# Rotary products on POOL, taken one in each step of the attention and put behind DVE's normalisation

## The chip, the cores and the metric

The kernel runs on one NeuronCore of a Trainium2 chip. It is one launch, and the metric is the device time of that launch in microseconds (us). Five engines work beside each other and wait for each other through semaphores: TensorE (PE in the profile), VectorE (DVE), ScalarE (ACT), GpSimd (POOL) and SyncE (SP), which issues the DMAs. Each engine takes its instructions in the order in which the program gives them to it.

## What is computed

The reference is an encoder block on 1024 tokens of width 1024 with two attention branches of eight heads each, a gate for each, and a squared-ReLU MLP. The change touches the windowed attention, in whose queries and keys the first 16 of each head's 64 values are rotated:

```python
qb = partial_rotary(qb.reshape(B, S, SWA_Q_HEADS, HEAD_DIM), pos)
kb = partial_rotary(kb.reshape(B, S, SWA_KV_HEADS, HEAD_DIM), pos)
y_na = neighbourhood_attention(qa, ka, va, na_rpb[l]) @ w_branch_na[l]
y_swa = windowed_gqa_with_sink(qb, kb, vb, swa_sink[l]) @ w_branch_swa[l]
mixed = jax.nn.sigmoid(ga) * y_na + jax.nn.sigmoid(gb) * y_swa
attn_out = mixed @ w_out[l] + b_out[l]
h = layer_norm(DEEPNORM_ALPHA * h + attn_out, ln1_g[l], ln1_b[l])
u = jnp.square(jax.nn.relu(h @ w_ff1[l] + b_ff1[l]))
h = layer_norm(DEEPNORM_ALPHA * h + u @ w_ff2[l] + b_ff2[l], ln2_g[l], ln2_b[l])
```

The rotation of a vector x is x * cos + swap(x) * sin, where swap exchanges the two halves of the 16 values.

## The kernel before

The work is held with channels on the 128 partitions and tokens along the free dimension. Products that need more than one pass of TensorE's number format are made of three matmuls, of a rounded part and a rest (names with hi or h, and lo or l). All engines run an order that is written by hand: the program text issues each instruction to its engine, and nothing moves it later.

**Steps.** The attention is a row of 64 steps, four for each of the 16 heads; a step is 256 queries, as two blocks of 128 queries against 256 or 384 keys. The first eight heads are the windowed ones. The work of a step is spread over three turns of the loop in `steps`, so that each engine always has something of another step at hand. Turn s issues, in this order:
- `part_a2` for step s + 1: DVE adds the sink to the sum of the exponentials (L563), takes the reciprocal (L564), and normalises the two blocks `ss` in place (L567, twice, 128x256 or 128x384);
- `part_a` for step s + 2: TensorE makes the two blocks of scores in a PSUM bank each (L530, L531; there are two such banks), DVE adds the mask and takes the row's maximum, writing the block `ss` (L533, twice, and a short read of the result each), and a small operation of two columns makes the bias of the exponential from it (L539);
- `part_b` for step s: TensorE transposes the normalised blocks, ACT rounds them to `pth` (L591), and DVE makes the rest `ptl` (L594). Between these two, `part_e` for step s + 2 lets ACT make the exponentials in place (L551, twice) and that of the sink (L554);
- `part_c` for step s - 1: TensorE multiplies with the values. In every second turn ACT (L630) and DVE (L631) bring the sum out of PSUM as `oT`.

**Fill.** Between these parts, `pump` gives TensorE matmuls of the projections (L278) that later heads need: 12 groups of three in each turn for the first eight heads. A list `later` holds what has to follow a projection; `defer` puts an entry on it with a number of groups to wait, and `flush` issues those that are due. The weights' rest (`wlo`, L486, DVE) and rounded part (`whi`, L481, ACT) come that way too.

**Rotary.** `rope` follows a half (512 tokens) of the projection of keys or of a pair of query heads. ACT brings it out of PSUM as `qf` (L393). Then `turn` issues four operations in a row: on DVE the swap, `stream_shuffle` into `qs` (L398), and on POOL the two products and the addition, each of 128x512 (L399, L400, L401). Some groups later `hi` (ACT, L437 for queries) and `lo` (DVE, L442, two instructions) make the rounded part and the rest. There are ten halves: two of the keys and two for each of four pairs of query heads. Five of them are turned ahead of the steps, and five inside them: the second half of the second pair, and both halves of the third and fourth. `qs` has one buffer (it shares the tag `vt`), and `qf` alternates between two.

POOL has nothing else to do in this stretch. Behind the steps here come the eight heads of neighbourhood attention, the gates, the output projection and the MLP.

Of the kernel before, what the change touches and what calls it, by code (L numbers as in the profile page):

```python
# [10 lines left out]
F32 = mybir.dt.float32  # L11
F32R = mybir.dt.float32r
AF = mybir.ActivationFunctionType
ALU = mybir.AluOpType

P = 128
# [62 lines left out]
SWAP = [(i + 8) % 16 if i < 16 else i for i in range(32)]  # L79
# [3 lines left out]
def encoder_block(ctx, tc, x, w_in, w_br, w_out, w_ff1, w_ff2, par, rows, rpbp,  # L83
                  ident_d, masks_d, rope_d, out):
    nc = tc.nc
    PE, ACT, DVE, POOL = nc.tensor, nc.scalar, nc.vector, nc.gpsimd

    def b32(ap):
        return ap.bitcast(F32)


    cp = ctx.enter_context(tc.tile_pool(name="const", bufs=1))
# [65 lines left out]
    ap = actx.enter_context(tc.tile_pool(name="ap", bufs=2, reuse_waits="tile"))  # L158
# [126 lines left out]
    def defer(*fns, pe=False):  # L285

        later.append([fns[0], fns[1:], pe])
# [75 lines left out]
    rt = ap.tile([P, 2, S], F32, tag="vv", name="rt")  # L363
# [17 lines left out]
        return bias_of  # L381

    n_rope = [0]

    def rope(ps, bias, half, then, late=D_ROPE):
        cs = slice(half * 512, (half + 1) * 512)
        b = []

        def evac():
            tag = ("x2", "wlo2")[n_rope[0] % 2]  # L390
            n_rope[0] += 1
            b.append((ap if tag == "x2" else wp).tile([P, 512], F32, tag=tag, name="qf", bufs=1))
            ACT.activation(b[0], ps, AF.Identity, bias=bias, scale=1.0)  # L393

        def turn():
            qf = b[0]
            qs = ap.tile([P, 512], F32, tag="vt", name="qs", bufs=1)
            DVE.stream_shuffle(qs, qf, SWAP)  # L398
            POOL.tensor_tensor(out=qf, in0=qf, in1=rt[:, 0, cs], op=ALU.mult)  # L399
            POOL.tensor_tensor(out=qs, in0=qs, in1=rt[:, 1, cs], op=ALU.mult)  # L400
            POOL.tensor_tensor(out=qf, in0=qf, in1=qs, op=ALU.add)  # L401
        hi, lo = then
        defer(0, evac, late[0], turn, late[1], lambda: hi(b[0]), late[2], lambda: lo(b[0]))

    def proj_swa_k(w, store):
        khs = [ap.tile([P, S], F32R, tag="kh", name="kh") for _ in range(2)]
        kls = [ap.tile([P, S], F32R, tag="kl", name="kl") for _ in range(2)]
        store.append((khs, kls))
        for half in range(2):
            ps = psum("mm")  # L410
            yield from gemm3_steps(ps, w, lambda part, k: h_perm(part, k, half))

            def hi(kf, half=half):
                for i in range(2):
                    a, b = slice(i * 64, i * 64 + 64), slice(64 - i * 64, 128 - i * 64)
                    ACT.copy(nat(khs[i][a], half), grp(kf[a]))
                    ACT.copy(nat(khs[i][b], half), grp(kf[a]))

            def lo(kf, half=half):
                for i in range(2):  # L420
                    a, b = slice(i * 64, i * 64 + 64), slice(64 - i * 64, 128 - i * 64)
                    DVE.tensor_tensor(out=nat(kls[i][a], half), in0=grp(kf[a]), in1=nat(b32(khs[i][a]), half),
                                      op=ALU.subtract)
                    DVE.tensor_copy(nat(kls[i][b], half), nat(b32(kls[i][a]), half))
            rope(ps, prm[:, C_KB:C_KB + 1], half, (hi, lo))

    def proj_swa_q(hp, w, store):
        qs = [ap.tile([P, S], F32R, tag="q", name="q", bufs=3) for _ in range(2)]
        store.extend(qs)
        for half in range(2):  # L430
            ps = psum("mm")
            yield from gemm3_steps(ps, w, lambda part, k: h_perm(part, k, half))

            def hi(qf, half=half):
                for i in range(2):
                    a = slice(i * 64, i * 64 + 64)
                    ACT.copy(nat(qs[i][a], half), grp(qf[a]))  # L437

            def lo(qf, half=half):
                for i in range(2):  # L440
                    a, b = slice(i * 64, i * 64 + 64), slice(64 - i * 64, 128 - i * 64)
                    DVE.tensor_tensor(out=nat(qs[i][b], half), in0=grp(qf[a]), in1=nat(b32(qs[i][a]), half),  # L442
                                      op=ALU.subtract)
            rope(ps, prm[:, C_QB + hp:C_QB + hp + 1], half, (hi, lo), D_ROPE2 if hp else D_ROPE)
# [111 lines left out]
    def part_a2(s):  # L556
        if s >= 64:
            return
        hd, t = heads[s // 4], s % 4
        pns, st = hd.pairs[t]  # L560
        sink_h = hd.get()[4]
        if sink_h is not None:
            DVE.tensor_tensor(out=st[:, 4:6], in0=st[:, 4:6], in1=st[:, 6:8], op=ALU.add)  # L563
        DVE.reciprocal(out=st[:, 6:8], in_=st[:, 4:6])  # L564
        for i in range(2):
            p, n, c0 = pns[i]
            DVE.tensor_scalar(out=p[:, :n], in0=p[:, :n], scalar1=st[:, 6 + i:7 + i], scalar2=None, op0=ALU.mult)  # L567

    def part_b(s, between):

        hd, t = heads[s // 4], s % 4
        pns = hd.pairs[t][0]

        order = []
        for c in range(max(2 * t - 1, 0), min(2 * t + 3, 8)):
            for i in range(2):
                if abs(2 * t + i - c) <= 1:
                    order.append((c, i))
        pth = ap.tile([P, 6, P], F32R, tag="pth", name="pth")
        ptl = ap.tile([P, 6, P], F32R, tag="ptl", name="ptl")  # L580
        cut = 3 if order[0][0] == 2 * t - 1 else 2
        pts = []
        for a, b in ((0, cut), (cut, len(order))):
            pt = psum("t")
            for u in range(a, b):
                c, i = order[u]
                p, n, c0 = pns[i]
                PE.transpose(pt[:, (u - a) * P:(u - a + 1) * P], p[:, (c - c0) * P:(c - c0 + 1) * P], ident)  # L588
            pts.append((a, b, pt[:, :(b - a) * P].rearrange("p (u f) -> p u f", f=P)))
        for a, b, pv in pts:  # L590
            ACT.copy(pth[:, a:b, :], pv)  # L591
        between()
        for a, b, pv in pts:
            DVE.tensor_tensor(out=ptl[:, a:b, :], in0=pv, in1=b32(pth[:, a:b, :]), op=ALU.subtract)  # L594
        hd.pairs[t] = order, pth, ptl
# [71 lines left out]
    with tc.manual_schedule(engines=MANUAL):  # L667
# [38 lines left out]
        for i in range(2 * NK + LAG + HB):  # L706
# [27 lines left out]
            for (h, w), lag in lags:  # L734
                j = i - lag - h * NK
# [15 lines left out]
        def steps(s, n, before_b=None, before_c=None):  # L751

            part = [int(n * SPLIT[0]), int(n * SPLIT[1])]
            part.append(n - sum(part))
            if 0 <= s + 1 < 64:
                part_a2(s + 1)
            if s + 2 < 64:
                part_a(s + 2)
            pump(part[0])
            if before_b:  # L760
                before_b()
            if 0 <= s < 64:
                part_b(s, lambda: part_e(s + 2))
            elif s < 0:
                part_e(s + 2)
            flush(False)
            pump(part[1])
            if before_c:
                before_c()
            if s >= 1:  # L770
                part_c(s - 1)
            flush()
            pump(part[2])
# [10 lines left out]
        def s1_sum(i):  # L784

            DVE.tensor_tensor(out=g1, in0=b32(hT[:, 0, K1, T2]) if i == 0 else g1,
                              in1=b32(hT[:, 0, K2, T2] if i == 0 else hT[:, 1, (K1, K2)[i - 1], T2]), op=ALU.add)
        counts = [CNT[0]] * 8 + [CNT[1]] * 8
        heads_w = []

        def head_w0(p):
# [390 lines left out]
    ops = {}  # L1182
# [840 lines left out]
```

## Time and profile before

| what | us |
|---|---|
| median of three runs (lowest, highest) | 1349.87 (1348.58, 1350.26) |
| the profiled execution, its own time | 1348.45 |
| its span on the core | 1346.7 |
| TensorE busy | 1321.3 |
| DVE busy | 993.5 |
| ACT busy | 707.4 |
| POOL busy | 278.9 |
| first and last shuffle L398 start | 53.6 and 178.9 |

A row of the timeline gives the start in us from the span's start, the time that the instruction took, the engine, the line, the operation, the tile that it writes and those that it reads, shapes and types, and how many were merged; in brackets stands how long the engine was idle before it and what ended that. Where two instructions are merged, the time is that from the start of the first to the end of the second. The ends of neighbours on one engine can overlap by about 0.1 us. A row of a list of waits gives who waited for whom, the us in total, the number of times, and the longest.

### The profile page before, as it was taken

How to read it: one execution, taken by the hardware profiler on the slowest of the kernel's cores; microseconds unless marked ns; L12 is line 12 of the kernel's file. 1: busy time of each engine (PE TensorE's matmuls, PEld its weight loads, DVE VectorE, ACT ScalarE, POOL GpSimd, SP SyncE). 2: the span in 40 equal slices, each digit the busy share in tenths (PEclk: the TensorE clock that was granted, in tenths of full speed). 3: DMA queues.
4: the chain of work that ended last, by engine and by line, in shares of the span. 5: the costliest groups of instructions: out<-in, count | busy, mean ns of one | idle time of the engine just before them, and what ended most of it. 6: DMA issues, size and time to landing. Idle time of an engine off the chain costs nothing.

```text
span 1346.7 us, 17318 instructions
## 1 busy us (share of the span) xinstructions
PE 1321.3 (98%) x6296; PEld 1087.7 (81%) x6296; DVE 993.5 (74%) x1617; ACT 707.4 (53%) x1230; POOL 278.9 (21%) x264
## 2 busy tenths in 40 slices
PE   8999999999999999999999999999999999999997
PEld 6788778888888878888888788888888888888785
DVE  7758988877777896443678977677655767787778
ACT  6446666766665545542446755555555533333346
POOL 4351121121120000334630012222100001011207
PEclk9999999999999999999999999999999999999999
DMA  6511111111101332655233566655628644544323
GB/s 230 196 69 48 48 51 41 38 38 44 38 23 39 126 126 103 214 195 198 79 141 133 179 228 203 211 194 181 207 99 304 219 188 149 211 148 176 121 102 125
DMA packets 66422, 183.94 MB, mean 137 GB/s; under 512 B 10400, under 2 KB 12064, under 8 KB 60576
## 3 DMA queue, kind: packets, MB, share of 16 engines
q1 hardware_dynamic: 65904, 182.38, 39.1%
q8 instruction: 49, 0.80, 0.2%
q10 hardware_dynamic: 432, 0.46, 0.1%
q14 instruction: 37, 0.30, 0.1%
HBM read 126.69 MB, written 56.31 MB: 136 GB/s over the span
## 4 chain that ended last, share of the span: by engine, by line
PE 73%; DVE 15%; ACT 7%; issue 2%; POOL 1%; DMA 1%; SPq 0%; DVEq 0%; ACTq 0%; POOLq 0%
PE ps_mm L278 10%; PE ps_mm L1746 6%; PE ps_o L1313 6%; PE ps_s L1746 6%; PE ps_t L1313 6%; PE ps_mm L1313 6%; PE ps_o L1746 5%; PE ps_t L1746 5%; ACT ss L551 3%; DVE ss L567 3%; PE ps_s L1313 2%; DVE ss L533 2%; PE ps_mm L851 1%; PE ps_o L624 1%; PE ps_t L588 1%
## 5 line engine op out<-in xcount | busy, mean ns | idle before, releaser
L278 PE MATMUL ps_mm<-hT,whi 128*128 128x512 f32 x832 | 270.0, 398 | 5.3 <-DVE kl L355 2.6
L278 PEld LDWEIGHTS ps_mm<-hT,whi 128*128 128x128 f32 x832 | 152.9, 188 | 35.3 <-DVE kl L355 4.6
L278 PE MATMUL ps_mm<-hT,wlo 128*128 128x512 f32 x416 | 166.9, 401 | 1.0 <-DVE wlo L684 1.0
L551 ACT ACTIVATE ss<-ss,st 128x384 f32<-128x384 f32 (+1 forms) x128 | 74.5, 585 | 79.9 <-DVE st L539 48.4
L1612 ACT CAST t<-stg 128x2048 fp32r<-128x2048 f32 x28 | 53.4, 1908 | 84.0 <-PE ps_o L1746 47.0
L1765 POOL TENSOR_TENSOR acc<-acc,rst 128x512 f32<-128x512 f32 x16 | 29.5, 1843 | 297.9 <-DMA rst<-xr_d 285.0
L1746 PE MATMUL ps_mm<-t,t 128*128 128x512 f32 x384 | 91.0, 392 | 0.0
L1746 PE MATMUL ps_s<-t,t 128*128 128x512 f32 x384 | 90.8, 392 | 0.0
L278 PEld LDWEIGHTS ps_mm<-hT,wlo 128*128 128x128 f32 x416 | 78.3, 188 | 12.2 <-DVE wlo L684 1.5
L1746 PEld LDWEIGHTS ps_mm<-t,t 128*128 128x128 f32 x384 | 72.1, 188 | 16.3
L1746 PEld LDWEIGHTS ps_s<-t,t 128*128 128x128 f32 x384 | 72.1, 188 | 16.1
L1313 PE MATMUL ps_t<-hS,tw 128*128 128x512 f32 x348 | 84.3, 391 | 0.0
L591 ACT CAST pth<-ps_t 128x384 fp32r<-128x384 f32 (+1 forms) x128 | 51.8, 455 | 52.5 <-PE ps_t L588 51.6
L1313 PEld LDWEIGHTS ps_t<-hS,tw 128*128 128x128 f32 x348 | 65.3, 188 | 14.3
L1615 DVE TENSOR_TENSOR t<-stg,t 128x2048 fp32r<-128x2048 f32 x28 | 65.5, 2338 | 13.1 <-ACT t L1612 13.1
L1135 POOL TENSOR_TENSOR mx<-sg 128x512 f32<-128x512 f32 x16 | 33.5, 2092 | 189.9 <-DVE sg L1134 189.9
L1746 PE MATMUL ps_t<-t,t 128*128 128x512 f32 x288 | 68.6, 392 | 0.4 <-DVE t L1615 0.3
L1746 PE MATMUL ps_o<-t,t 128*128 128x512 f32 x288 | 67.8, 391 | 0.0
L594 DVE TENSOR_TENSOR ptl<-ps_t,pth 128x384 fp32r<-128x384 f32 (+1 forms) x128 | 61.1, 518 | 7.0 <-ACT pth L591 6.8
L1746 PEld LDWEIGHTS ps_t<-t,t 128*128 128x128 f32 x288 | 53.9, 188 | 13.1 <-DVE t L1615 1.3
L1746 PEld LDWEIGHTS ps_o<-t,t 128*128 128x128 f32 x288 | 54.1, 188 | 11.8
L1589 POOL TENSOR_TENSOR rst<-rst,rr 128x512 f32<-128x512 f32 x16 | 22.6, 1412 | 190.7 <-DMA rst<-xn_d 190.7
(306 smaller groups left out, 3170.5 us busy)
## 6 DMA issues: line engine op xcount, KB each, us to landing
us_d<-usl SPq DMA_DIRECT2D x112, 256.0 KB
stg<-us_d SPq DMA_DIRECT2D x28, 1024.0 KB
raw<-in_w_ff SPq DMA_DIRECT2D x36, 512.0 KB
raw<-in_w_in SPq DMA_DIRECT2D x28, 512.0 KB
sg<-sg_d SPq DMA_DIRECT2D x32, 256.0 KB
w2b<-in_w_ff SPq DMA_DIRECT2D x7, 1024.0 KB
w2a<-in_w_ff SPq DMA_DIRECT2D x5, 1024.0 KB
sg_d<-sa SPq DMA_DIRECT2D x16, 256.0 KB
```

The costliest lines, as they stand in the source:

```text
L278: PE.matmul(ps, a[:, k, :], act(b, k), start=(k == 0 and i == 0), stop=(k == NK - 1 and i == 2))
L533: DVE.tensor_tensor_reduce(out=p[:, :n], in0=ps[:, :n], in1=bias_of(j), scale=1.0, scalar=NEG, op0=ALU.add, op1=ALU.max, accum_out=st[:, i ...
L551: ACT.activation(p[:, :n], p[:, :n], AF.Exp, bias=st[:, 2 + i:3 + i], scale=0.125, accum_out=st[:, 4 + i:5 + i])
L567: DVE.tensor_scalar(out=p[:, :n], in0=p[:, :n], scalar1=st[:, 6 + i:7 + i], scalar2=None, op0=ALU.mult)
L591: ACT.copy(pth[:, a:b, :], pv)
L594: DVE.tensor_tensor(out=ptl[:, a:b, :], in0=pv, in1=b32(pth[:, a:b, :]), op=ALU.subtract)
L1135: POOL.tensor_tensor(out=mx[:, f, half * 512:(half + 1) * 512], in0=both[0], in1=both[1], op=ALU.add)
L1313: PE.matmul(ps, ww, act[:, part, k, :], start=(first and k == 0 and m == 0), stop=(k == 3 and m == 2), skip_group_check=True)
L1612: ACT.copy(slot[:, :, 0, :], src)
L1615: DVE.tensor_tensor(out=slot[:, :, 1, :], in0=src, in1=b32(slot[:, :, 0, :]), op=ALU.subtract)
L1746: PE.matmul(ps, st[:, a, part, j * P:(j + 1) * P], w[:, a, wpart, :], start=(first and a == 0 and m == 0), stop=(a == 3 and m == 2), skip_ ...
L1765: POOL.tensor_tensor(out=z, in0=z, in1=t, op=ALU.add)
```

## The change

Inside the steps, `turn` no longer issues its four operations at once. It puts five entries on a list `rope_ops`: the shuffle, the two products, the addition, and an entry that defers `hi` and `lo`. If the list holds nothing else, the shuffle is issued at once. At the end of each `part_a2` the new function `rope_step` takes one product or addition from the list. Ahead of it stands a copy on POOL of one column of the block that DVE normalised last, into a small tile `junk`, so POOL's queue waits there for the second L567 of that step. After an addition, `hi` is deferred by 4 groups, and if a second half is on the list, its shuffle by 8. Ahead of the steps the order is as it was.

```diff
--- before.py
+++ after.py
@@ -381,6 +381,18 @@
         return bias_of
 
     n_rope = [0]
+    in_steps, rope_ops = [], []
+
+    def rope_step(p):
+
+        if rope_ops:
+            j = cp.tile([P, 1], F32, tag="junk", name="junk", bufs=2)
+            POOL.tensor_copy(j, p[:, 0:1])
+            rope_ops.pop(0)()
+            if len(rope_ops) % 5 == 1:
+                rope_ops.pop(0)()
+                if rope_ops:
+                    defer(8, rope_ops.pop(0))
 
     def rope(ps, bias, half, then, late=D_ROPE):
         cs = slice(half * 512, (half + 1) * 512)
@@ -394,13 +406,25 @@
 
         def turn():
             qf = b[0]
-            qs = ap.tile([P, 512], F32, tag="vt", name="qs", bufs=1)
-            DVE.stream_shuffle(qs, qf, SWAP)
-            POOL.tensor_tensor(out=qf, in0=qf, in1=rt[:, 0, cs], op=ALU.mult)
-            POOL.tensor_tensor(out=qs, in0=qs, in1=rt[:, 1, cs], op=ALU.mult)
-            POOL.tensor_tensor(out=qf, in0=qf, in1=qs, op=ALU.add)
+            qs = []
+
+            def shuffle():
+                qs.append(ap.tile([P, 512], F32, tag="vt", name="qs", bufs=1))
+                DVE.stream_shuffle(qs[0], qf, SWAP)
+            ops = [shuffle,
+                   lambda: POOL.tensor_tensor(out=qf, in0=qf, in1=rt[:, 0, cs], op=ALU.mult),
+                   lambda: POOL.tensor_tensor(out=qs[0], in0=qs[0], in1=rt[:, 1, cs], op=ALU.mult),
+                   lambda: POOL.tensor_tensor(out=qf, in0=qf, in1=qs[0], op=ALU.add),
+                   lambda: defer(4 if in_steps else late[1], lambda: hi(qf), late[2], lambda: lo(qf))]
+            if in_steps:
+                rope_ops.extend(ops)
+                if len(rope_ops) == 5:
+                    rope_ops.pop(0)()
+            else:
+                for op in ops:
+                    op()
         hi, lo = then
-        defer(0, evac, late[0], turn, late[1], lambda: hi(b[0]), late[2], lambda: lo(b[0]))
+        defer(0, evac, late[0], turn)
 
     def proj_swa_k(w, store):
         khs = [ap.tile([P, S], F32R, tag="kh", name="kh") for _ in range(2)]
@@ -565,6 +589,7 @@
         for i in range(2):
             p, n, c0 = pns[i]
             DVE.tensor_scalar(out=p[:, :n], in0=p[:, :n], scalar1=st[:, 6 + i:7 + i], scalar2=None, op0=ALU.mult)
+        rope_step(p)
 
     def part_b(s, between):
 
@@ -786,6 +811,7 @@
             DVE.tensor_tensor(out=g1, in0=b32(hT[:, 0, K1, T2]) if i == 0 else g1,
                               in1=b32(hT[:, 0, K2, T2] if i == 0 else hT[:, 1, (K1, K2)[i - 1], T2]), op=ALU.add)
         counts = [CNT[0]] * 8 + [CNT[1]] * 8
+        in_steps.append(1)
         heads_w = []
 
         def head_w0(p):
```

Lines after the change have other numbers: L398 to L401 become L413 and L415 to L417, L442 becomes L466, L486 L510, L533 L557, L539 L563, L563 and L564 L587 and L588, L567 L591, L594 L619, and L631 L656. So an L563 in the rows of the change is the small operation that makes the bias.

POOL's queue at the sixth and seventh half, the first ones inside the steps, before:

```order
L399 TENSOR_TENSOR qf<-qf,rt 128x512
L400 TENSOR_TENSOR qs<-qs,rt 128x512
L401 TENSOR_TENSOR qf<-qf,qs 128x512
L399 TENSOR_TENSOR qf<-qf,rt 128x512
L400 TENSOR_TENSOR qs<-qs,rt 128x512
L401 TENSOR_TENSOR qf<-qf,qs 128x512
```

and with the change:

```order
L390 COPY junk<-ss 128x1
L415 TENSOR_TENSOR qf<-qf,rt 128x512
L390 COPY junk<-ss 128x1
L416 TENSOR_TENSOR qs<-qs,rt 128x512
L390 COPY junk<-ss 128x1
L417 TENSOR_TENSOR qf<-qf,qs 128x512
L390 COPY junk<-ss 128x1
L415 TENSOR_TENSOR qf<-qf,rt 128x512
```

The order of the products is the same; a copy that reads `ss` stands ahead of each of the fifteen. They go into the steps 1 to 3, 7 to 12 and 15 to 20, counted by the step that is normalised.

DVE's queue where the second half of the third pair of query heads is swapped (`wlo` is a weight's rest, `oT` the output of a head), the end of one step and the end of the next, before:

```order
L539 TENSOR_SCALAR st<-st,snk_101 128x2
L594 TENSOR_TENSOR ptl<-ps_t,pth 128x384
L594 TENSOR_TENSOR ptl<-ps_t,pth 128x256
L398 STREAM_SHUFFLE qs<-qf 128x512
L563 TENSOR_TENSOR st<-st 128x2
L564 RECIPROCAL st<-st 128x2
```

and one step later on DVE:

```order
L539 TENSOR_SCALAR st<-st,snk_101 128x2
L594 TENSOR_TENSOR ptl<-ps_t,pth 128x256
L594 TENSOR_TENSOR ptl<-ps_t,pth 128x384
L486 TENSOR_TENSOR wlo<-raw,whi 128x1024
L631 TENSOR_TENSOR oT<-ps_o,oT 64x512
L563 TENSOR_TENSOR st<-st 128x2
```

and with the change:

```order
L563 TENSOR_SCALAR st<-st,snk_101 128x2
L619 TENSOR_TENSOR ptl<-ps_t,pth 128x384
L619 TENSOR_TENSOR ptl<-ps_t,pth 128x256
L587 TENSOR_TENSOR st<-st 128x2
L588 RECIPROCAL st<-st 128x2
```

and one step later on DVE:

```order
L563 TENSOR_SCALAR st<-st,snk_101 128x2
L619 TENSOR_TENSOR ptl<-ps_t,pth 128x256
L619 TENSOR_TENSOR ptl<-ps_t,pth 128x384
L510 TENSOR_TENSOR wlo<-raw,whi 128x1024
L656 TENSOR_TENSOR oT<-ps_o,oT 64x512
L413 STREAM_SHUFFLE qs<-qf 128x512
L587 TENSOR_TENSOR st<-st 128x2
```

The shuffle left the step without `wlo` and `oT` and stands one step later, behind them. The same happens in the fourth pair.

DVE's queue where the rest `q` of that half is made, before:

```order
L539 TENSOR_SCALAR st<-st,snk_101 128x2
L594 TENSOR_TENSOR ptl<-ps_t,pth 128x384
L594 TENSOR_TENSOR ptl<-ps_t,pth 128x256
L442 TENSOR_TENSOR q<-qf,q 64x4x16x8 x2
L563 TENSOR_TENSOR st<-st 128x2
L564 RECIPROCAL st<-st 128x2
```

and one step later on DVE:

```order
L539 TENSOR_SCALAR st<-st,snk_101 128x2
L594 TENSOR_TENSOR ptl<-ps_t,pth 128x256
L594 TENSOR_TENSOR ptl<-ps_t,pth 128x384
L486 TENSOR_TENSOR wlo<-raw,whi 128x1024
L631 TENSOR_TENSOR oT<-ps_o,oT 64x512
L563 TENSOR_TENSOR st<-st 128x2
```

and with the change:

```order
L563 TENSOR_SCALAR st<-st,snk_101 128x2
L619 TENSOR_TENSOR ptl<-ps_t,pth 128x384
L619 TENSOR_TENSOR ptl<-ps_t,pth 128x256
L587 TENSOR_TENSOR st<-st 128x2
L588 RECIPROCAL st<-st 128x2
```

and one step later on DVE:

```order
L563 TENSOR_SCALAR st<-st,snk_101 128x2
L619 TENSOR_TENSOR ptl<-ps_t,pth 128x256
L619 TENSOR_TENSOR ptl<-ps_t,pth 128x384
L510 TENSOR_TENSOR wlo<-raw,whi 128x1024
L466 TENSOR_TENSOR q<-qf,q 64x4x16x8 x2
L656 TENSOR_TENSOR oT<-ps_o,oT 64x512
L587 TENSOR_TENSOR st<-st 128x2
```

The two instructions that write `q` went one step later, between `wlo` and `oT`; ACT's two casts for them moved along. The same happens in the fourth pair. The other instructions of DVE, ACT and TensorE, and all DMAs, keep their order.

## The prediction

> **What bounds the kernel now.** I read the profile's chain that ended last first, then its piece between 80 and 210 us, because the rotary products that the change moves run there: five of the ten halves are turned inside the attention steps.
>
> ```profile
> PE 73%; DVE 15%; ACT 7%; issue 2%; POOL 1%; DMA 1%; SPq 0%; DVEq 0%; ACTq 0%; POOLq 0%
> by line: DVE ss L567 20.4%; DVE ss L533 15.8%; ACT ss L551 15.2%; DVE q L442 7.1%; DVE oT L631 5.3%; issue 4.6%; ACT oT L630 4.6%; DVE st L539 4.5%; DVE ptl L594 3.9%; DVE st L564 3.1%; DVE st L563 2.7%; POOL qf L401 2.7%; POOL qs L400 2.3%
> PE ps_s L530 <- DVE st L533: 4.2, 8, 1.0
> ```
>
> The first line is the whole span: TensorE carries 73% of the chain. The second is the piece from 80 to 210 us: there the chain is almost all DVE and ACT, and L567, the normalisation, has the largest share. The third is the list of waits from 90 to 260 us: TensorE idles 4.2 us in eight waits of L530 for a bank that DVE's L533 frees. So in these twenty-odd steps a loop runs the kernel: L539 gives the bias, ACT makes the exponentials, DVE takes L563, L564, L567, two L533, and the next L539. What lengthens that loop lengthens the span.
>
> How much TensorE can gain at most I take from the starts of L530 in its timeline.
>
> ```profile
> 101.80 0.44 PE L530 MATMUL ps_s<-kh,q 128*128 128x384 f32 x1 [0.19 <-DVE st L533]
> ...
> 112.61 0.34 PE L530 MATMUL ps_s<-kh,q 128*128 128x384 f32 x1
> ...
> 131.46 0.34 PE L530 MATMUL ps_s<-kh,q 128*128 128x384 f32 x1
> ...
> 208.37 0.38 PE L530 MATMUL ps_s<-kh,q 128*128 128x256 f32 x1 [0.73 <-DVE st L533]
> ```
>
> From 112.61 to 131.46 are four steps with no wait: 18.85 us, 4.71 each. From 101.80 to 208.37 are 21 steps: 106.57 us instead of 21 x 4.71 = 98.9. So 7.6 us are lost on TensorE, and no more than that is to be had.
>
> **What the change removes.** POOL's burst of three products stands beside DVE's normalisation five times. One of the five, POOL and DVE:
>
> ```profile
> 128.06 1.28 POOL L399 TENSOR_TENSOR qf<-qf,rt 128x512 f32<-128x512 f32 x1 [27.01 <-DVE st L563]
> 129.31 1.40 POOL L400 TENSOR_TENSOR qs<-qs,rt 128x512 f32<-128x512 f32 x1
> 130.79 1.30 POOL L401 TENSOR_TENSOR qf<-qf,qs 128x512 f32<-128x512 f32 x1
> 98.69 2.57 DVE L567 TENSOR_SCALAR ss<-ss,st 128x384 f32<-128x384 f32 x2
> 128.19 2.67 DVE L567 TENSOR_SCALAR ss<-ss,st 128x384 f32<-128x384 f32 x2
> 139.14 2.84 DVE L567 TENSOR_SCALAR ss<-ss,st 128x384 f32<-128x384 f32 x2
> 169.23 2.69 DVE L567 TENSOR_SCALAR ss<-ss,st 128x384 f32<-128x384 f32 x2
> 180.16 2.53 DVE L567 TENSOR_SCALAR ss<-ss,st 128x384 f32<-128x384 f32 x2
> 119.39 0.75 DVE L567 TENSOR_SCALAR ss<-ss,st 128x384 f32<-128x384 f32 x2
> 110.04 0.68 DVE L567 TENSOR_SCALAR ss<-ss,st 128x384 f32<-128x384 f32 x2
> ```
>
> The pair of L567 that starts at 128.19 ends at 130.86, just after L400 ends and L401 starts: it got through where POOL's products left room. Undisturbed, a pair takes 0.75 us (0.68 where its second is 128x256, as at 128.19 and 169.23). The excess is 1.82 + 1.99 + 2.09 + 2.01 + 1.78 = 9.69 us. Small operations are held too:
>
> ```profile
> 97.14 1.30 POOL L399 TENSOR_TENSOR qf<-qf,rt 128x512 f32<-128x512 f32 x1 [3.15 <-DVE qs L398]
> 97.97 0.49 DVE L563 TENSOR_TENSOR st<-st 128x2 f32<-128x2 f32 x1 [0.91 <-ACT st L554]
> 165.15 0.14 DVE L563 TENSOR_TENSOR st<-st 128x2 f32<-128x2 f32 x1
> 131.71 0.40 DVE L539 TENSOR_SCALAR st<-st,snk 128x2 f32<-128x2 f32 x1
> 171.84 1.28 POOL L401 TENSOR_TENSOR qf<-qf,qs 128x512 f32<-128x512 f32 x1
> 172.77 0.38 DVE L539 TENSOR_SCALAR st<-st,snk 128x2 f32<-128x2 f32 x1
> ```
>
> L563 took 0.49 us instead of 0.14, and L539 0.40 and 0.38 instead of 0.23 (below). Each of the three ends within 0.04 us of POOL's instruction beside it: 98.46 after 98.44, 132.11 after 132.09, 173.15 after 173.12. That is 0.35 + 0.17 + 0.15 = 0.67 us more. **Removed: 10.36 us** of DVE's part of the loop.
>
> **What it adds, first: fifteen waits of L539.** Each product now starts after the second L567 of a step, with one small copy ahead. DVE's next operations there are the two L533, which stood beside L401 at 130.78 unharmed:
>
> ```profile
> 130.78 0.41 DVE L533 CUSTOM_DVE_ANT_0 ss<-ps_s,bd 128x256 f32<-128x256 f32 x1
> 131.13 0.55 DVE L533 CUSTOM_DVE_ANT_0 ss<-ps_s,bd 128x384 f32<-128x384 f32 x1
> 126.11 0.23 DVE L539 TENSOR_SCALAR st<-st,snk 128x2 f32<-128x2 f32 x1
> 124.51 0.75 DVE L567 TENSOR_SCALAR ss<-ss,st 128x384 f32<-128x384 f32 x2
> 121.12 0.23 DVE L539 TENSOR_SCALAR st<-st,snk 128x2 f32<-128x2 f32 x1
> 22.83 0.27 POOL L212 TENSOR_SCALAR mv<-mv 128x1 f32<-128x1 f32 x1
> 23.06 1.27 POOL L250 TENSOR_TENSOR hT<-t,hT 128x512 fp32r<-128x512 f32 x1
> 96.33 0.73 DVE L398 STREAM_SHUFFLE qs<-qf 128x512 f32<-128x512 f32 x1
> 127.19 0.73 DVE L398 STREAM_SHUFFLE qs<-qf 128x512 f32<-128x512 f32 x1
> ```
>
> But then comes L539. Call T the end of the second L567. With a 128x256 block among the L533, T is 124.51 + 0.75 = 125.26 and L539 ends at 126.34, T + 1.08; with two 128x384 (119.39 and 121.12) it ends at T + 1.21. POOL follows DVE by 0.08 us (shuffle's end 97.06, L399 at 97.14) to 0.14 (127.92 and 128.06). Its copy of one column is not in this trace. The nearest is L212, which holds POOL 0.23 us to the start of the next; I bound the copy by 0.10 and 0.27 and take 0.20. The product takes 1.29 (between 1.28, and 1.40 as L400 at 129.31). It ends at T + 0.11 + 0.20 + 1.29 = T + 1.60, and L539 0.02 later. That is 0.54 late in eight steps and 0.41 in seven: 8 x 0.54 + 7 x 0.41 = **7.2 us added**. With the short ends (0.08 + 0.10 + 1.28) the waits sum to 5.1 us, with the long ones (0.14 + 0.27 + 1.40) to 10.3. All of it is on the loop: ACT's exponentials wait for L539's result, and L594 stands behind it on DVE.
>
> By the Trainium skill, page "SBUF — State Buffer", section "Who interferes with whom", DVE and GpSimd have one pair of ports in common, which is locked for a whole instruction, and a tensor_scalar can contend for it while a DVE operation with a single SBUF input outside the two-port modes does not. The trace agrees (L533 0.41 us unharmed, L539 0.40 instead of 0.23), so by that rule the sum stays; were a tensor_scalar of two columns outside those modes, this 7.2 would be nothing. [...]
>
> **Second: work moved into fuller steps.** The second half's shuffle, twice, leaves a step in which DVE waited for ACT anyway and goes behind L631 in the step that also has a weight split:
>
> ```profile
> 143.90 1.22 DVE L486 TENSOR_TENSOR wlo<-raw,whi 128x1024 fp32r<-128x1024 f32 x1
> 145.36 0.68 DVE L631 TENSOR_TENSOR oT<-ps_o,oT 64x512 f32<-64x512 f32 x1 [0.24 <-ACT oT L630]
> 146.06 0.16 DVE L563 TENSOR_TENSOR st<-st 128x2 f32<-128x2 f32 x1
> 158.59 1.39 DVE L442 TENSOR_TENSOR q<-qf,q 64x512 fp32r<-64x512 f32 x2
> 154.75 1.25 ACT L437 CAST q<-qf 64x512 fp32r<-64x512 f32 x2
> 160.15 0.73 ACT L591 CAST pth<-ps_t 128x256 fp32r<-128x256 f32 x2
> 204.53 0.67 ACT L304 ACTIVATE vt<-ps_mm,prm 128x512 f32<-128x512 f32 x1
> ```
>
> L563 follows L631 at once there (146.06), so the shuffle adds its 0.73 us: 2 x 0.73 = 1.46. The pair of L442 (1.39 us), also twice, moves one step later, into a step that has the split of 1.22 us and L631. The first time, ACT's casts (1.25, in front of its 0.73 of L591) and then L594, 1.22, 1.39 and 0.68 one after another on DVE put L563 about 1.5 us later than 165.15, and about half of the 1.39 comes back from the emptied step: I take 0.85. The second time ACT is late in that step by 0.67 us of L304 anyway, and I take 0.25. Together **2.6 us added**; if the wait of DVE for ACT covers it all, nothing.
>
> TensorE's instructions keep their order, and no DMA moves. The copies' own wait costs nothing: behind it on POOL stand only the products, and what waits for those, the second half's shuffle and the casts to `q`, is issued a step or more after the last of them. The shuffle's tile, held longer, is next written some two steps after the last addition.
>
> **Sum:** 10.36 - 7.2 - 2.6 = 0.6 us gained. The profiled execution took 1348.45 us (span 1346.7); the median of the three runs is 1349.87. Behind 210 us nothing changes, so what is won or lost there stays: **1347.9 for the profiled run, 1349.3 us against the median**. Ends: 10.36 - 5.1 - 0 = 5.3 gained, 10.36 - 10.3 - 2.6 = 2.5 lost: 1344.6 to 1352.4.
>
> **The rivals.**
>
> A. The stall goes and none takes its place: L539 is not held, or only where the product happens to start early. For it: it is an operation of two columns, and the rows that show it held are two. Against it: both end with POOL. Then 10.36 - 2.6 = 7.8 us come off the loop, and TensorE's 7.6 caps them; 0.73 of those stand at 208.37, after the products. 6.9 us gained: 1343.0. Chance 0.15.
>
> B. Slower: POOL's product, alone in its step, still lasts as it did in the stage before, where DVE's operations interrupted it.
>
> ```profile
> 90.87 1.75 POOL L400 TENSOR_TENSOR qs<-qs,rt 128x512 f32<-128x512 f32 x1
> ```
>
> With 1.75 us it ends at T + 2.06, L539 is 0.94 late (against the mean end T + 1.14), 15 x 0.94 = 14.1, and 10.36 - 2.6 - 14.1 is 6.3 us lost: 1356.2. It decides from (10.36 - 2.6) / 15 = 0.52 us a step: a wait above that makes the change a loss. Against it: the additions at 130.79 and 171.84, with L539 waiting, took 1.30 and 1.28. Chance 0.12.
>
> **How the numbers follow.** My forecast has 0.73, the rivals 0.15 and 0.12. The range takes the forecast's ends, 1344.6 to 1352.4, a little wider for a run's own spread (1348.58 to 1350.26), and reaches into A to leave out no more than 0.2: 1344.0 to 1352.8. A difference of 0.2%, 2.7 us, is about what a measurement of this kernel can tell from none. Faster than 1347.17: A's 0.15 and 0.06 of the forecast's short waits, 0.21. Slower than 1352.57: B's 0.12 and 0.02, 0.14. Between: 0.65.
>
> **What would show it.** In the profile after, all pairs of the normalisation between 98 and 182 us should be 0.68 to 0.75 us. L539 should take some 0.65 to 0.8 us in fifteen steps, ending with POOL's product; if it stays at 0.23, A is right. POOL's products should be 1.28 to 1.30; at 1.75, B is. The shuffles at two places should stand behind L631 with L563 0.7 us later. L530 for the step that started at 208.37 should start near 207.8. I am wrong if the loop was not the bound (stalls go and L530 does not move), or if the copy costs far from 0.2 us.

## The result and the profile after

| what | before | after |
|---|---|---|
| median, us (lowest, highest) | 1349.87 (1348.58, 1350.26) | 1337.84 (1337.20, 1340.32) |
| the profiled execution, its own time | 1348.45 | 1338.99 |
| its span | 1346.7 | 1337.2 |
| TensorE busy | 1321.3 | 1310.3 |
| DVE busy | 993.5 | 986.3 |

The ratio is 0.9916, with a 95% interval of 0.9902 to 0.9931: about 12 us faster. The forecast was 1349.3 in a range of 1344.0 to 1352.8. The time lies 6 us under the range.

The views that the prediction used are these, after the change: the chain of the whole span by engine, the chain between 80 and 210 us by line, and TensorE's wait for a scores' bank between 90 and 260 us (us in total, times, longest).

```profile
PE 74%; DVE 14%; ACT 7%; issue 2%; POOL 1%; DMA 1%; SPq 0%; DVEq 0%; ACTq 0%; POOLq 0%
```

```profile
by line: ACT ss L575 13.6%; DVE ss L557 12.9%; DVE ss L591 9.4%; DVE st L563 6.7%; DVE q L466 6.2%; PE ps_mm L278 5.4%; DVE oT L656 5.2%; issue 4.4%; ACT oT L655 3.6%; DVE qs L413 3.4%; DVE ptl L619 3.4%; POOL qf L417 2.7%; DVE st L588 2.6%
```

```profile
PE ps_s L554 <- DVE st L557: 3.3, 4, 1.5
```

In the steps the normalisation (L591 now) has fallen from 20.4% of the chain to 9.4%, and the bias operation (L563 now) has risen from 4.5% to 6.7%. TensorE waits 3.3 us instead of 4.2. That is a small change. TensorE's own timeline at L554, which makes the scores, tells how small:

```profile
95.59 0.33 PE L554 MATMUL ps_s<-kh,q 128*128 128x384 f32 x1
...
103.08 0.33 PE L554 MATMUL ps_s<-kh,q 128*128 128x384 f32 x1
...
167.18 0.39 PE L554 MATMUL ps_s<-kh,q 128*128 128x256 f32 x1 [1.16 <-DVE st L557]
...
208.25 0.39 PE L554 MATMUL ps_s<-kh,q 128*128 128x256 f32 x1 [1.52 <-DVE st L557]
```

From the step that started at 101.80 before to the one at 208.37 were 106.57 us. Now they are 208.25 - 103.08 = 105.17: 1.40 us gained. The first of the five bursts stood ahead of that, beside the pair of L567 at 98.69. Ahead of every moved product lies this step of before:

```profile
93.95 0.33 PE L530 MATMUL ps_s<-kh,q 128*128 128x384 f32 x1
```

From it to the one at 208.37 were 114.42 us, and are 208.25 - 95.59 = 112.66: 1.76 gained in all. That it starts 1.64 later now, with the same order ahead of it, I put down to the start of a run: in two other executions of the change's beginning it starts at 94.85 and 96.67. **The rest is behind the products.** From the start at 208 to the end of the span were 1346.7 - 208.37 = 1138.33 us, and are 1337.2 - 208.25 = 1128.95: 9.38 us of the 9.5 by which the two spans differ; the later start and the gain in the steps nearly cancel. There the order of every engine is what it was.

The table by stretches shows that part of the kernel. Each row gives the stretch, its length, and then the busy time with the number of instructions for PE, its weight loads, DVE, ACT and POOL; then the granted clock, the DMA share and GB/s. Before:

```profile
600.00:750.00 150.00, 150.00 (x684) 122.44 (x683) 102.27 (x144) 70.98 (x121) 52.40 (x45) 1.00 0.37 134
750.00:900.00 150.00, 148.47 (x647) 120.97 (x646) 114.80 (x156) 84.50 (x147) 30.21 (x20) 1.00 0.64 212
900.00:1050.00 150.00, 150.00 (x657) 123.02 (x656) 96.01 (x119) 80.68 (x124) 17.25 (x12) 1.00 0.56 193
1050.00:1200.00 150.00, 149.95 (x653) 122.14 (x652) 110.55 (x82) 59.09 (x40) 13.09 (x8) 1.00 0.50 186
```

and after:

```profile
600.00:750.00 150.00, 150.00 (x695) 124.58 (x694) 103.32 (x146) 71.74 (x123) 52.09 (x45) 1.00 0.39 137
750.00:900.00 150.00, 148.51 (x655) 122.35 (x654) 114.49 (x158) 86.73 (x151) 32.22 (x22) 1.00 0.64 212
900.00:1050.00 150.00, 150.00 (x663) 124.11 (x662) 97.00 (x118) 80.93 (x123) 15.54 (x11) 1.00 0.58 198
1050.00:1200.00 150.00, 149.40 (x660) 123.38 (x659) 110.89 (x81) 58.02 (x38) 15.88 (x8) 1.00 0.49 184
```

TensorE is busy nearly all the time in both, at a granted clock of 1.00 in both. But in the same 600 us it gets through 695 + 655 + 663 + 660 = 2673 matmuls instead of 684 + 647 + 657 + 653 = 2641. It hardly waits in either; each matmul takes less. In the timeline of the MLP's matmuls, 24 in a row are merged:

```profile
1033.54 5.60 PE L1746 MATMUL ps_s<-t,t 128*128 128x512 f32 x24
1038.98 5.61 PE L1746 MATMUL ps_t<-t,t 128*128 128x512 f32 x24
1044.43 5.60 PE L1746 MATMUL ps_o<-t,t 128*128 128x512 f32 x24
1049.87 5.76 PE L1746 MATMUL ps_mm<-t,t 128*128 128x512 f32 x24
1055.47 5.76 PE L1746 MATMUL ps_s<-t,t 128*128 128x512 f32 x24
```

Before, some rows of 24 take 5.60 us and others 5.76. After, they take 5.60 to 5.66:

```profile
1032.57 5.60 PE L1772 MATMUL ps_t<-t,t 128*128 128x512 f32 x24
1038.01 5.60 PE L1772 MATMUL ps_o<-t,t 128*128 128x512 f32 x24
1043.45 5.66 PE L1772 MATMUL ps_mm<-t,t 128*128 128x512 f32 x24
1048.94 5.60 PE L1772 MATMUL ps_s<-t,t 128*128 128x512 f32 x24
```

Which rows are slow is found from the program. The SBUF addresses of a matmul's operands are fixed in it. Some tiles are laid from the left end of SBUF, the others from the right. Before the change the left ones start at byte 416 modulo 512 (416 more than a multiple of 512) of a partition and the right ones at 480. The two `junk` tiles take 32 bytes each at the left, and move every left tile behind them by 64 bytes: both sides are at 480 then. I took all neighbouring 128x512 matmuls behind the attention, and grouped the time from the start of one to the start of the next by the distance from the address of its moving operand to that of the weights, modulo 512:

```
                 distance   matmuls   mean ns
before                  0      1568     227.6
before                 64       973     233.2   moving left, weights right
before                448      1225     229.4   moving right, weights left
after                   0      3763     226.9
```

Against 226.9 that is 973 x 6.3 + 1225 x 2.5 + 1568 x 0.7 = 6.1 + 3.1 + 1.1 = 10.3 us, a little more than the 9.4 of the spans. The rows of 5.60 us shown from before are at a distance of 0, the two of 5.76 at 64. Those at 0 have either both operands on the left, at 416, or both on the right, at 480, and the two kinds follow each other alike, every 227.4 to 227.5 ns: it is the distance that counts, and not the place itself. (A matmul's own weights and those of the next are at the same distance nearly always in this kernel, so which of the two counts can't be told here.)

### The profile page after: what moved, and what is told of

Read it like the earlier page. It is cut to its first block, busy times and chain, and to the rows that moved or that the text cites. A ratio compares the mean times of both kernels' runs of the same rounds, so it can differ in the third digit from the quotient of the medians.

```text
span 1337.2 us, 17345 instructions
## 1 busy us (share of the span) xinstructions
PE 1310.3 (98%) x6296; PEld 1087.5 (81%) x6296; DVE 986.3 (74%) x1617; ACT 707.7 (53%) x1230; POOL 283.2 (21%) x279
## 4 chain that ended last, share of the span: by engine, by line
PE 74%; DVE 14%; ACT 7%; issue 2%; POOL 1%; DMA 1%; SPq 0%; DVEq 0%; ACTq 0%; POOLq 0%
PE ps_mm L278 11%; PE ps_mm L1772 6%; PE ps_o L1339 6%; PE ps_s L1772 6%; PE ps_t L1339 6%; PE ps_mm L1339 6%; PE ps_o L1772 5%; PE ps_t L1772 5%; PE ps_s L1339 2%; ACT ss L575 2%; DVE ss L557 2%; PE ps_o L649 2%; DVE ss L591 1%; PE ps_mm L877 1%; PE ps_t L613 1%
## 5 line engine op out<-in xcount | busy, mean ns | idle before, releaser
L619 DVE TENSOR_TENSOR ptl<-ps_t,pth 128x384 fp32r<-128x384 f32 (+1 forms) x128 | 61.1, 516 | 7.0 <-ACT pth L616 6.5
```

## The experiments

Two theories stood after this. **P**: the 64 bytes, and so the placement of the operands, make about 10 us, and the moved products about 1. **S**: the moved products make all of it, and TensorE's faster stretch behind them follows in some way from that. The first four kernels below shared one chip, the next four another, each with runs of the kernel before; every ratio is to those.

**The placement alone.** The kernel before, with an unused tile of 64 bytes:

```diff
         t = cp.tile([P, 4, 8], F32, name="rrow")
+        pad = cp.tile([P, 16], F32, name="pad")
+        POOL.memset(pad, 0.0)
```

> The kernel before, with 64 bytes per partition more in the const pool (one unused tile, one memset), so that every tile on the left side of the SBUF lies 64 bytes further on, as in the changed kernel; its schedule is that of before. Theory P (placement: the matmuls behind the attention are faster because moving operand and weights now lie at the same offset modulo some power of two): about 9.6 us less than before, 1340, and the matmuls at L1746 start every 227 ns. Theory S (the order of the rotary products brought the time, in the attention or later): no change, 1349.9, with matmuls at L1746 every 227 to 234 ns as before.

Measured: 1338.92 us (1338.66 to 1339.28) against 1349.41, ratio 0.992 [0.9905, 0.9935]. 10.5 us are gained with no instruction of the attention moved. The first of the four stretches has 696 matmuls, against the change's 695:

```profile
600.00:750.00 150.00, 150.00 (x696) 124.81 (x695) 103.76 (x146) 71.72 (x122) 52.41 (x45) 1.00 0.39 138
```

**The schedule alone.** The change, with POOL's copy written into a column of a tile that is dead by then, so that no tile moves:

```diff
+        rr_t.append(t)
...
-            j = cp.tile([P, 1], F32, tag="junk", name="junk", bufs=2)
-            POOL.tensor_copy(j, p[:, 0:1])
+            POOL.tensor_copy(rr_t[0][:, 0, 0:1], p[:, 0:1])
```

> The changed kernel with its copies written into a tile that is dead by then (the small tile of the residual rows), so no tile moves against before. Theory P: only what the steps gained stays, 1 to 2 us less than before, 1348 to 1349, and the matmuls behind the attention are as slow as before (227 to 234 ns). Theory S: as the changed kernel, 1337.8.

Measured: 1348.24 us (1347.32 to 1348.66) against 1349.41, ratio 0.999 [0.998, 0.9999]: 1.2 us gained, with an interval from 0.1 to 2.7. The stretch is back at the 684 of before:

```profile
600.00:750.00 150.00, 150.00 (x684) 122.47 (x683) 102.00 (x144) 70.64 (x121) 52.38 (x45) 1.00 0.37 134
```

P is shown, and S falls: 10.5 + 1.2 = 11.7 of the 12.0 us. In this run's trace TensorE took 208.76 - 95.48 = 113.28 us for the steps that were 114.42 before, 1.1 less.

**Which distances are slow.** The kernel before with pads of other sizes (48, 8 and 80 columns in place of 16) puts the two sides at other distances.

> The kernel before with 192 bytes more. If what counts is the offset modulo 128 bytes or less, as e1_pad64: about 1340. If it is modulo 256 or 512, the sides differ (by 128) and it is slower than e1_pad64, by 3 us or more. Theory S: 1349.9.

> The kernel before with 32 bytes more: left and right side then differ by 32 bytes modulo 64. Theory P in its plain form (equal offsets are fast, unequal ones slow): slower than e1_pad64 by 5 us or more. If instead it was only the boundary of 64 bytes that the left tiles had to get off, it cannot be told beforehand: both sides were at 32 modulo 64 before and after. Theory S: 1349.9.

> The kernel before, with 320 bytes of unused tile ahead of its left side instead of 64, and one memset of it (the unused tile is all that is added; nothing is left out). The two sides' offsets then differ by 256 bytes modulo 512, and by nothing modulo 256. Theory M512 (the matmul is quick only where its two operands' addresses agree modulo 512): the matmuls on operands of different sides take 232 to 234 ns as with 128 and 192 bytes, and the time is 1350 to 1354 us. Theory M256 (agreement modulo 256 is enough): they take 227 to 229 ns, and the time is 1338 to 1340 us as with 64 bytes.

The times were 1352.64 with 192 bytes (ratio 1.0023 [1.0013, 1.0032]), 1353.51 with 32 (1.0028 [1.0018, 1.0038]) and 1339.49 with 320 (0.9922 [0.9908, 0.9935]). The same stretch, for 192, 32 and 320 bytes:

```profile
600.00:750.00 150.00, 150.00 (x684) 122.80 (x683) 100.15 (x142) 68.95 (x117) 52.40 (x45) 1.00 0.38 138
```

```profile
600.00:750.00 150.00, 150.00 (x682) 122.41 (x681) 99.81 (x141) 68.73 (x117) 52.52 (x46) 1.00 0.38 139
```

```profile
600.00:750.00 150.00, 150.00 (x696) 124.83 (x695) 104.21 (x146) 71.07 (x122) 52.38 (x45) 1.00 0.39 138
```

and the spacing of the matmuls between the two sides, worked out as above:

```
pad, bytes   moving left, weights right    moving right, weights left
             distance   mean ns            distance   mean ns
none               64     233.2                 448     229.4
192               384     232.7                 128     233.1
32                 32     233.2                 480     233.4
320               256     226.8                 256     226.8
```

A distance of 256 is as quick as none; 32, 128, 384 and 480 cost some 6 ns, and so does 64. Of those tried only 448 is cheaper, 2.5 ns. So agreement modulo 256 is enough, and modulo 128 it isn't. Why 448 costs less than 64 is open, and so is why the matmuls at a distance of 0 are themselves some 0.7 ns slower in the kernels that have slow ones.

**What the waits of the bias operation cost.** Here the question is the prediction's own sum. The copy, and the product behind it, now follow the bias operation instead of the normalisation, in the change:

```diff
@@ part_a, behind the bias operation (L563)
+        rope_step(st[:, 2:4])
@@ part_a2, behind the normalisation (L591)
-        rope_step(p)
```

> The change, with POOL's copy and product put behind DVE's bias operation (L563, two columns) instead of behind the normalisation; nothing is left out and no tile moves. Theory W (the fifteen waits of that operation, 0.64 us instead of 0.23, stand on the loop that sets a step's length): the operation is at 0.23 us again, and the steps give back up to 15 x 0.41 = 6.1 us, of which 2 to 3 are kept, since the products now end 0.3 later and hold the low bits, the q pair or the shuffle instead: 1334.5 to 1336.5 us. Theory N (the waits lie beside ACT's work and cost nothing): 1337.5 to 1339 us, no change against the change itself.

Measured: 1334.27 us (1333.93 to 1334.67), ratio 0.9883 [0.9869, 0.9896]. This beats both kernels: 3.6 us under the change's 1337.84, and the intervals of the ratios don't meet. The gain is a little larger than theory W had it (1334.5 to 1336.5). The groups of DVE between 90 and 210 us (instructions, busy us, mean ns, idle us), with the change:

```profile
L591 DVE TENSOR_SCALAR ss<-ss,st 128x384 f32<-128x384 f32 x35 | 13.8, 423 | 0.6
L563 DVE TENSOR_SCALAR st<-st,snk 128x2 f32<-128x2 f32 x24 | 11.8, 491 | 0.9
L466 DVE TENSOR_TENSOR q<-qf,q 64x512 fp32r<-64x512 f32 x14 | 10.8, 770 | 0.5 <-ACT q L461 0.2
L510 DVE TENSOR_TENSOR wlo<-raw,whi 128x1024 fp32r<-128x1024 f32 x6 | 7.3, 1212 | 0.0
...
L591 DVE TENSOR_SCALAR ss<-ss,st 128x256 f32<-128x256 f32 x11 | 3.9, 350 | 0.2
```

and with this edit:

```profile
L466 DVE TENSOR_TENSOR q<-qf,q 64x512 fp32r<-64x512 f32 x14 | 11.6, 828 | 0.3
L510 DVE TENSOR_TENSOR wlo<-raw,whi 128x1024 fp32r<-128x1024 f32 x6 | 9.4, 1568 | 0.0
...
L563 DVE TENSOR_SCALAR st<-st,snk 128x2 f32<-128x2 f32 x25 | 5.8, 233 | 0.9
```

The bias operation is at 233 ns: 11.8 - 24 x 0.23 = 6.3 us of waits are gone. In their place the weight's rest (L510) takes 9.4 - 7.3 = 2.1 us more and `q` (L466) 0.8 more, because POOL's product now stands beside them. One such place, on POOL and on DVE:

```profile
138.50 1.30 POOL L417 TENSOR_TENSOR qf<-qf,qs 128x512 f32<-128x512 f32 x1
```

```profile
138.93 1.94 DVE L510 TENSOR_TENSOR wlo<-raw,whi 128x1024 fp32r<-128x1024 f32 x1
```

The net is 6.3 - 2.9 = 3.4 us, close to what the time shows: 3.6 against the change's 1337.84, and 3.2 against the 1337.50 of its repetition below. So what DVE is held in these steps goes into the time nearly whole. TensorE's steps agree: 203.68 - 102.33 = 101.35 us instead of 105.17.

```profile
102.33 0.33 PE L554 MATMUL ps_s<-kh,q 128*128 128x384 f32 x1
...
203.68 0.38 PE L554 MATMUL ps_s<-kh,q 128*128 128x256 f32 x1 [1.31 <-DVE st L557]
```

**The same cost from the other side.** POOL's copy takes 128 columns instead of one, so each product starts later:

```diff
-            j = cp.tile([P, 1], F32, tag="junk", name="junk", bufs=2)
-            POOL.tensor_copy(j, p[:, 0:1])
+            j = cp.tile([P, 144], F32, tag="junk", name="junk", bufs=1)
+            POOL.tensor_copy(j[:, 0:128], p[:, 0:128])
```

> The change, with POOL's copy widened from 1 column to 128 (one junk tile of 144 columns instead of two of 1; the address of every left tile moves by a whole 512 bytes, so matmul rates stay; nothing is left out). The copy, 0.19 us, becomes 0.25 to 0.45, and every product of POOL ends that much later. Theory W: the bias operation's fifteen waits grow by that and the time with them: each 0.1 us of copy costs up to 15 x 0.1 = 1.5 us, so 1339 to 1342 us. Theory N: only the waits grow, the time stays at 1337.5 to 1339 us.

Measured: 1339.56 us (1339.05 to 1341.23), ratio 0.9925 [0.9912, 0.9937]. POOL's copies, and DVE's bias operation between 90 and 210 us:

```profile
L390 POOL COPY junk<-ss 128x128 f32<-128x128 f32 x15 | 4.4, 290 | 81.3 <-DVE ss L591 81.3
```

```profile
L563 DVE TENSOR_SCALAR st<-st,snk 128x2 f32<-128x2 f32 x23 | 13.5, 586 | 0.8
```

The copy takes 290 ns instead of 185. Less 0.23 for each, the waits of the fifteen are 13.5 - 23 x 0.23 = 8.2 us, 1.9 more than with the change. The time is 1.7 us above its 1337.84, but the intervals of the two ratios overlap. The steps tell more: 211.31 - 104.16 = 107.15 us, 1.98 more than the change's. This distance, from the step at 101.80 before, varies little from one execution to the next: it is 106.3 to 106.6 in the traces of the five kernels with the order of before (before itself and the four pads), and 105.17 and 207.85 - 102.74 = 105.11 in the change and its repetition. So W holds here too, by the steps; the times alone would not show it.

```profile
104.16 0.33 PE L554 MATMUL ps_s<-kh,q 128*128 128x384 f32 x1
...
211.31 0.39 PE L554 MATMUL ps_s<-kh,q 128*128 128x256 f32 x1 [1.55 <-DVE st L557]
```

**The fuller steps.** Two numbers of the change's planning, so that the two instructions for `q` go into the step that the shuffle left:

```diff
-                   lambda: defer(4 if in_steps else late[1], lambda: hi(qf), late[2], lambda: lo(qf))]
+                   lambda: defer(hi_at.pop(0) if in_steps else late[1], lambda: hi(qf), late[2], lambda: lo(qf))]
```

with `hi_at = [4, 4, 0, 4, 0]`.

> The change, with the q pair of the two late fills put back in the steps that the moved shuffle emptied, instead of one step later beside the low bits and the eviction; nothing is left out and no tile moves. Theory F (work that stands in fuller steps costs what I summed for it, twice 0.85 + 0.25 less what the other step hides): 0.8 to 1.5 us faster than the change, 1336.5 to 1337.5 us. Rival: a step is set by the loop over ACT and PE and not by what DVE has left, so where the pair stands costs nothing: within 0.3 us of the change, 1337.5 to 1338.5 us.

Measured: 1341.39 us (1339.87 to 1341.62), ratio 0.9933 [0.992, 0.9947]. Both expectations missed: it was to be faster or the same. The time is 3.6 us above the change's, but the intervals of the two ratios overlap. TensorE's steps, which varied by no more than 0.3 us at an unchanged order, take 211.33 - 102.45 = 108.88 us, 3.7 more than the change's.

```profile
102.45 0.33 PE L555 MATMUL ps_s<-kh,q 128*128 128x384 f32 x1
...
211.33 0.28 PE L555 MATMUL ps_s<-kh,q 128*128 128x256 f32 x1
```

The timeline of POOL, ACT and DVE in the emptied step shows why:

```profile
155.41 1.28 POOL L418 TENSOR_TENSOR qf<-qf,qs 128x512 f32<-128x512 f32 x1
```

```profile
158.15 1.04 ACT L506 CAST whi<-raw 128x1024 fp32r<-128x1024 f32 x1
159.09 1.26 ACT L462 CAST q<-qf 64x512 fp32r<-64x512 f32 x2
```

```profile
159.74 1.39 DVE L467 TENSOR_TENSOR q<-qf,q 64x512 fp32r<-64x512 f32 x2 [2.24 <-ACT q L462]
```

POOL's addition ends at 156.69. ACT's cast for `q` stands behind its cast of a weight, 1.04 us, and DVE, with nothing of its own to do ahead of `q`, waits 2.24 us. Before the change ACT made that cast a step earlier (154.75), which is now too early: the sum isn't there yet. So this run did not undo the term that I meant to measure; it made a new wait.

**The change again, and both edits together.** These two shared one chip.

> The change itself, unchanged, once more, so that it stands beside the next run on one chip. All theories: 1337.2 to 1340.3 us, as in its five runs.

> The change with both edits: POOL's copy behind DVE's bias operation, and the q pair put back in the emptied steps; nothing is left out and no tile moves. If the earlier pair is bad wherever the copy stands (in the trace of the pair alone DVE waits 2.24 us for ACT's q, which has a 1.04 us cast of raw ahead of it): 2 to 3 us over the version with the copy alone (1334.27 us), so 1336 to 1337.5 us, still under the change. If it was bad only because products end late: 1333 to 1334.5 us.

The change: 1337.50 us (1337.33 to 1338.20), ratio 0.9913 [0.99, 0.9927]. With both edits: 1337.28 us (1336.77 to 1337.67), ratio 0.991 [0.9896, 0.9923]. The early pair costs 3.0 us with the copy behind the bias operation too (in TensorE's steps 207.83 - 102.81 = 105.02 us instead of 101.35, 3.7 more), and DVE waits there for ACT's `q` 4.5 us in all, so the first expectation holds. The best kernel is the one with the copy alone moved.

## Why the prediction was wrong

- **The step that failed** is "Behind 210 us nothing changes, so what is won or lost there stays". Of the difference of the spans 9.4 us lie there. The order of the instructions indeed didn't change, but the two `junk` tiles moved the left tiles by 64 bytes, and the matmuls of operands from different sides went from 229.4 and 233.2 ns to 226.9. The sum has no term for the new tiles at all. The prediction asked what the copy costs POOL and never where its result lies. No single row of the profile of before said it, but the rows of 24 matmuls at 5.60 and 5.76 us without a wait between them were there to be seen.
- **What was to go** went as summed. The normalisation's two groups fell from 27.4 to 17.7 us between 90 and 210 us, 9.7 us; the prediction's five excesses were 9.69. All pairs between 98 and 182 us take 0.68 to 0.75 us now, as the prediction asked. Before:

```profile
L567 DVE TENSOR_SCALAR ss<-ss,st 128x384 f32<-128x384 f32 x35 | 21.5, 642 | 0.6
...
L567 DVE TENSOR_SCALAR ss<-ss,st 128x256 f32<-128x256 f32 x11 | 5.9, 538 | 0.2
```

- **The fifteen waits** were there, each ending with POOL's product, and were somewhat shorter: 6.3 us instead of 7.2. One of them, on POOL and DVE:

```profile
129.68 0.18 POOL L390 COPY junk<-ss 128x1 f32<-128x1 f32 x1 [17.17 <-DVE ss L591]
129.82 1.28 POOL L415 TENSOR_TENSOR qf<-qf,rt 128x512 f32<-128x512 f32 x1
```

```profile
128.94 0.68 DVE L591 TENSOR_SCALAR ss<-ss,st 128x384 f32<-128x384 f32 x2
...
130.47 0.66 DVE L563 TENSOR_SCALAR st<-st,snk 128x2 f32<-128x2 f32 x1
```

  The product starts 0.14 us behind the start of the copy, where I had taken 0.20, and it ends at 131.10; L563 ends at 131.13. The copy itself is 0.18 to 0.19. The Trainium skill, page "SBUF — State Buffer", section "Who interferes with whom", counts `tensor_scalar` among the operations of DVE that can take the pair of ports shared with GpSimd, and lets the one that comes second wait for a whole instruction; the trace agrees, at 0.54 to 0.74 us instead of 0.23.
- **The fuller steps**, 2.6 us, were not measured by themselves. 10.36 - 6.3 less the 1.8 us that the steps gained leaves 2.3, so the size is not contradicted, but this is what is left of a sum, and how it divides between shuffle and `q` is open. Part of it stands in DVE's groups between 90 and 210 us: ahead of the operation that starts a normalisation (L563 before, L587 after) DVE idles 2.8 us more, nearly all of it for ACT. Ahead of `oT` it idles 1.0 less (7.5 and 6.5 us). Before and after:

```profile
L563 DVE TENSOR_TENSOR st<-st 128x2 f32<-128x2 f32 x23 | 3.9, 169 | 3.3 <-ACT st L554 2.9
```

```profile
L587 DVE TENSOR_TENSOR st<-st 128x2 f32<-128x2 f32 x23 | 3.5, 153 | 6.1 <-ACT st L578 6.0
```

  One place on the other side is in the rows of the result: TensorE waits 1.16 us up to 167.18, behind a step in which DVE makes the weight's rest, `q` and `oT` one after another.
- **The sum for the schedule**, 0.6 us gained, measured 1.2 (0.1 to 2.7) with the tiles held in place; TensorE's steps gained 1.1 in that run and 1.8 with the change. The 1348.24 lies in the range. The mechanism of this part was right: the stall went and the fifteen waits came. Its size is borne out only within these bounds, and the third term was not measured, so that the sum came so near is in part luck.
- **Rival A** (the bias operation isn't held) and **rival B** (products of 1.75 us) are both refuted by the rows above: L563 is held, and the product takes 1.28. A's time, 1343.0, was nearest to what came, but not for A's reason.
- The point that L530's step would start near 207.8 came out at 208.25 in the profiled run, which began 1.64 late. Less that it is 206.6, 1.8 earlier than before where about 0.6 was forecast.

## What to carry to other kernels

A change that adds, drops or resizes a tile moves the tiles behind it, and where TensorE is busy all the time, a few ns for each of thousands of matmuls can outweigh a schedule, as here: compare the operands' addresses before and after, and hold them fixed (or pad) when a schedule is to be judged. Count matmuls per stretch where PE shows 100% busy, since busy time alone says nothing of their rate. And where one engine's instruction holds another's, put it beside operations that aren't held by it, and price the step by what it then meets: here 6.3 us were exchanged for 2.9.

## What the runs showed of the hardware

Matmuls of 128x512 whose moving operand and weights lie at the same address modulo 256 bytes followed each other every 226.8 to 227.6 ns; at distances of 32, 64, 128, 384 and 480 every 232.7 to 233.4, and at 448 every 229.4. The granted clock was 1.00 in these stretches. The Trainium skill, page "SBUF — State Buffer", section "Who interferes with whom", lets only the port pair of DVE and GpSimd cause contention and calls the reads of the moving operand and of the weights independent; the measurement differs from that, in that the place of one in relation to the other sets the rate. That the cause lies in how SBUF serves the two reads is a guess: the runs show the dependence on the addresses, not what makes it.
